# A recurrent layer and an attention layer on one core: the order in the last pass of a group of heads, and the place of the weight loads, changed

## The chip, the cores and the metric

The kernel runs on one core of a Trainium2 chip. The core has a matrix engine (PE, TensorE) that loads a 128x128 block of weights and streams up to 512 columns past it, a vector engine (DVE), a scalar engine for functions and casts (ACT), a general engine (POOL) and a sync engine (SP), which here issues all the transfers (DMAs). Each engine works through its own list of instructions in a fixed order, and an instruction that waits for a semaphore holds everything behind it on its engine. The metric is the device time of one execution in microseconds; less is better.

## The reference

One sequence of 1024 tokens with 1024 features goes through two layers with residuals: an RG-LRU layer and a layer of forgetting attention with 16 heads of 64 features, then a final norm. The change lies in the attention layer:

```python
def fox_mixer(h, w_in, b_f, w_out):
    u = h @ w_in
    q, k, v = (u[..., i * 1024:(i + 1) * 1024] for i in range(3))   # 16 heads x 64
    gate = u[..., 3 * 1024:4 * 1024]
    f_logit = u[..., 4 * 1024:] + b_f
    cum = cumsum(log_sigmoid(f_logit), axis=1)
    logits = q @ k.T / 8 + (cum_q - cum_k)       # for each head, causal mask
    p = softmax(logits)
    y = (p @ v) * silu(gate)
    return y @ w_out
```

All numbers are float32. The kernel gets that accuracy from three products of a reduced format: each operand is split into a high part (a cast) and a low part (what the cast left over), and high*high, low*high and high*low are added up in PSUM.

## The kernel before, in words

**Names.** A weight block is loaded from memory into a buffer `wf` (three such buffers exist), cast by ACT into its high part `wh`, and DVE subtracts to get the low part `wl`; after that the `wf` buffer is free again. `gps` are the products of the projections to queries, keys and gates (128 weights by 512 tokens), `vps` those of the values (128 tokens by 256 value columns, that is four heads), `S` the logits, `pt` transposed probabilities, and `O` the probabilities times the values. `ph` and `pl` are the high and low part of probabilities, `p` and `pp` rows of probabilities. Some of the probabilities are transposed on PE (`pt`); the others go out to memory and come back turned (`turnd<-turn`, then `pp<-turnd`), and their `ph` and `pl` are read from `pp`.

**Heads, passes and groups.** The attention runs head by head. Each head has two passes, for the two halves of the queries: `weigh(hd, 0)` runs beside `maxima(hd, 1)`, and `weigh(hd, 1)` beside `maxima(hd + 1, 0)`. `maxima` makes logits, masks them on DVE (line 775), and takes the exponential on ACT (line 780). `weigh` turns the probabilities, splits them and multiplies them with the values. Two heads are a pair, and share blocks of queries, keys and gates; four heads are a group, and share a block of values. While one pair is worked on, the projections of the next pair are made as a filling: `kq_units` for queries and keys and `g_units` for gates, through `project`, which makes four steps of six products for each half of the tokens. In the last head of a group (heads 3, 7 and 11) the values of the next group are prepared: `value_weights` loads and splits their weights, and `values` makes 192 products.

**The order.** Strings of digits and dots set it: a digit takes a step of one of the two passes, a dot takes a step of the filling (`fill`) and one of the small side work (`side`). The first pass of a head has five dots and the second six; heads 12 to 15 use longer strings (`LAST`). What is left of the filling is taken when the pass is over. The strings give each instruction its place in the program, and some instructions get an explicit "issue after". A scheduler with a model of the times then sets the real order on each engine: it moves what has no such tie, such as loads, weight splits and products of the values, to where its model finds the engine idle.

```python
ORDER = "1.0..1.10.1.0", "10..1.0.10.10.0"
LAST = "1..0.1..10..1..0", "10..1.0..10..1.0..0"
...
            run(second, weigh(hd, 1), maxima(hd + 1, 0), fill=fill, side=side)
            drain(side)
...
            if hd < 12:
                drain(fill)
            if hd % 4 == 3 and hd < 12:
                drain(values(hd // 4 + 1, parts))
```

Of the kernel before, what the change touches and what calls it, by code (L numbers as in the profile page):

```python
# [17 lines left out]
P = 128  # L18
# [20 lines left out]
def trunk(ctx: ExitStack, tc: tile.TileContext, xt, w0, wg, wo0, pc, gn, gf, w1, wv, wf, bf, wo1, out):  # L39
# [73 lines left out]
    def weights(src, parts=wpool, lo_eng=nc.gpsimd):  # L113

        for k in range(0, src.shape[1], 4):
            n = min(4, src.shape[1] - k)
            yield from split_weights([(src[:, k : k + n], slice(0, P))], (n, P), nc.scalar, lo_eng, parts)

    def gemm_steps(ps, pairs, chunks=(slice(0, HALF),)):

        pairs = list(pairs)
        for cs in chunks:
            o = ps[:, cs]
            for i, ((wh, wl), (xh, xl)) in enumerate(pairs):
                matmul(o, wh, xh[:, cs], start=i == 0, stop=False)
                matmul(o, wl, xh[:, cs], start=False, stop=False)
                matmul(o, wh, xl[:, cs], start=False, stop=i == len(pairs) - 1)
                if i % 2:
                    yield

    def drain(gen):
        for _ in gen:
            pass
# [368 lines left out]
    with ExitStack() as l1:  # L502
# [14 lines left out]
                    nc.vector.memset(f32(u[64:, 1]), 0.0)  # L517
                    nc.vector.memset(f32(u[64:68, 1]), -1.0)

        def project(w, use, hs=(0, 1)):  # L520

            for h in hs:
                pt = ps.tile([P, HALF], F32, tag="g", name="gps1")
                yield from gemm_steps(pt, zip(w, hT[h]))
                use(h, pt)

        def value_weights(g, parts):
# [20 lines left out]
        def values(g, parts):  # L548

            ex = 0 if g else HEADS  # L550
            for k in range(0, 0 if g else KT, 2):
                src = [(wv[g, :, k : k + 2], slice(0, 256)), (wf[:, k : k + 2], slice(256, 256 + ex))]
                parts += split_weights(src, (2, 256 + ex), nc.scalar, nc.gpsimd)
                if k == 2:
                    yield
            Vs[2 * g], Vs[2 * g + 1] = [], []
            for st in range(8):
                if ex and st % 2:
                    pt = ps.tile([P, SEQ], F32, tag="S", name="vps")[:, : 256 + ex]
                else:  # L560
                    pt = ps.tile([P, 256 + ex], F32, tag="g", name="vps")
                c = (st % 4) * P
                for k in range(KT):
                    xh, xl = hT[st // 4][k]
                    wh, wl = parts[k]
                    xh, xl = xh[:, c : c + P], xl[:, c : c + P]
                    matmul(pt, xh, wh, start=k == 0, stop=False)
                    matmul(pt, xl, wh, start=False, stop=False)
                    matmul(pt, xh, wl, start=False, stop=k == KT - 1)
                    if k % 4 == 1:  # L570
                        yield
                r_ = rms1[st // 4][:, st % 4 : st % 4 + 1]
                for a in range(2):
                    v = vpool.tile([P, 4, HD], F32R, tag=f"v{st}", name=f"v{st}", bufs=2)
                    src = pt[:, a * P : (a + 1) * P].rearrange("p (b d) -> p b d", b=2)
                    to_hi(v[:, 0::3], src, nc.scalar, scale=r_)
                    nc.vector.scalar_tensor_tensor(v[:, 1:3], src, r_, f32(v[:, 0::3]), ALU.mult, ALU.subtract)
                    Vs[2 * g + a].append(v)
                if ex:
                    nc.vector.tensor_scalar(fz[:, st], pt[:, 256:], r_, None, ALU.mult)  # L580
# [7 lines left out]

        kqw = {}

        def low(pair):
            return nc.vector if pair else nc.gpsimd

        def kq_units(pair, parts=((1, (0, 1)), (0, (0, 1)))):

            for is_k, hs in parts:
                if hs[0] == 0:
                    kq[pair, is_k] = tuple(
                        kqpool.tile([P, SEQ], F32R, tag=f"qk{p}{is_k}", name=f"qk{p}") for p in "hl"
                    )  # L600
                if hs[0] == 0 or pair == 0:
                    kqw[is_k] = list(weights(w1[is_k * 8 + pair], lo_eng=low(pair)))
                hi, lo = kq[pair, is_k]
                eng = nc.vector if pair == 0 else nc.scalar

                def use(h, pt):
                    cs = halves[h]
                    nc.vector.tensor_tensor(pt, pt, rs1[h], ALU.mult)
                    if is_k:
                        to_hi(hi[:, cs], pt, eng)  # L610
                        to_lo(lo[:, cs], pt, hi[:, cs], nc.vector)
                    else:
                        to_hi(hi[:, cs], pt, eng, scale=0.125)
                        nc.vector.scalar_tensor_tensor(lo[:, cs], pt, 0.125, f32(hi[:, cs]), ALU.mult, ALU.subtract)

                yield from project(kqw[is_k], use, hs)

        def load(hd, cs=slice(0, SEQ), us=(0, 1)):

# [72 lines left out]
        def g_units(pair, hs=(0, 1)):  # L692

            if hs[0] == 0:
                sgs[pair] = at.tile([P, SEQ], F32, tag="sg", name="sg1")
                gw[0] = list(weights(w1[16 + pair], lo_eng=low(pair)))
            sg = sgs[pair]

            def use(h, pt):
                g_ = sg[:, h * HALF : (h + 1) * HALF]  # L700
                nc.vector.tensor_tensor(g_, pt, rs1[h], ALU.mult)
                t = at.tile([P, HALF], F32, tag="xp", name="t1", bufs=2)
                nc.scalar.activation(t, g_, AF.Tanh, scale=0.5)
                nc.vector.scalar_tensor_tensor(g_, t, 1.0, g_, ALU.add, ALU.mult)

            yield from project(gw[0], use, hs)

        stats, ps_ = {}, {}

# [244 lines left out]
        def beside(*gens):  # L954
            for _ in itertools.zip_longest(*gens):
                yield
# [5 lines left out]
        def chain(*gens):  # L962
            for g in gens:
                yield from g
# [11 lines left out]
        def run(order, *gens, **kw):  # L976

            ordered(order, *gens, **kw)
            for g in gens:
                drain(g)  # L980
# [146 lines left out]
        for hd in range(HEADS):  # L1127
            pair = hd // 2
            if hd % 2 == 0:
                if hd < 12:  # L1130
                    fill = kq_units(pair + 1, ((1, (0, 1)), (0, (0,))))
                elif hd == 12:
                    pairs = ((0, 1), (2, 3), (4, 5), (6, 7))
                    todo = [(db, c) for two in pairs for c in range(2) for db in two]
                    fill = chain(
                        kq_units(7),
                        g_units(7, (0,)),
                        load_y(0),
                        first_out(),
                        g_units(7, (1,)),  # L1140
                        load_y(1),
                        partial(todo),
                        turned(0, 0),
                        turned(0, 1),
                    )
            elif pair < 6:
                fill = chain(kq_units(pair + 1, ((0, (1,)),)), late_q(hd + 1), g_units(pair + 1))
            first, second = LAST if hd > 11 else ORDER
            side = put_away(hd - 1) if 0 < hd < 13 else iter(())
            if hd % 4 == 3 and hd < 12:  # L1150
                parts = []
                coming = value_weights(hd // 4 + 1, parts)
                side = beside(side, itertools.islice(coming, 5))
            run(first, weigh(hd, 0), maxima(hd, 1), fill=fill, side=side)
            drain(side)
            if hd == HEADS - 1:
                break
            if hd == 14:
                with tc.issue_after(seen[0].ins):
                    split_y(1, 6, yos[6, 1])  # L1160
                scale(hd)
            side = late() if hd == 14 else settle(hd)
            if hd % 4 == 3 and hd < 12:
                side = beside(side, coming)
            run(second, weigh(hd, 1), maxima(hd + 1, 0), fill=fill, side=side)
            drain(side)
            if hd > 11:
                gated(hd, 1)
            if hd == 13:
                with tc.issue_after(seen[0].ins):  # L1170
                    split_y(0, 6, yos[6, 0])
            if hd < 12:
                drain(fill)
            if hd % 4 == 3 and hd < 12:
                drain(values(hd // 4 + 1, parts))
            if hd + 2 < HEADS:
                load(hd + 2, us=(0,) if hd % 2 == 0 and hd < 12 else (0, 1))
        quarters = [slice(0, 256), slice(256, HALF)]
# [83 lines left out]
```

## Time and profile before

| what | us |
|---|---|
| median of 3 runs (lowest, highest) | 1113.85 (1109.61, 1116.99) |
| the profiled execution, its own time | 1113.33 |
| its span, from the first instruction to the last | 1111.6 |
| PE busy with products | 1088.2 |
| PE busy with loading weights, beside the products | 921.9 |
| DVE busy | 785.4 |
| ACT busy | 581.3 |
| POOL busy | 175.2 |

The attention's heads begin at about 520 us of the span and end near 1050; the last passes of the three groups lie at about 604 to 647, 747 to 790 and 889 to 931 us. The 1.7 us between the profiled execution's own time and its span lie before the first and after the last instruction.

A row of the timeline gives the start in us from the span's beginning, the duration, the engine, the source line, the operation, what is written and read, the shape, how many such instructions were merged, and in brackets the idle time of the engine before it with what ended it. Most products show line 57, most casts line 87, most subtractions line 98, because helpers record them. PE overlaps its products, so that the duration of one (0.39 us for 512 columns) is longer than the distance to the next (0.23 us): the distance between two starts is what a product costs. A row of the windows gives the stretch in us, then its length, the busy time of PE, weight loading, DVE, ACT and POOL with the number of their instructions, the granted clock of PE as a share of the full one, the busy share of the DMA engines, and GB/s.

### The profile page before, as it was taken

The page shows a single profiled execution, that of the slowest core. Times are in us where ns is not written, and L with a number is a line of the kernel's source. Part 1 is how long each engine was busy: PE and PEld are TensorE (multiplying, and loading weights), DVE is VectorE, ACT ScalarE, POOL GpSimd, SP SyncE. Part 2 cuts the span into 40 slices and gives each one's busy share as a digit, 9 for nine tenths or more (in the row PEclk, how much of TensorE's full clock was granted, in tenths as well). Part 3 has the DMA queues.
Part 4 walks back from the last instruction along what each step waited for, and adds up shares of the span by engine and source line. Part 5 has one row for each costly group of instructions (what it writes and reads, how often), then busy time and mean ns, then how long its engine had stood idle before and what let it go on. Part 6 is the DMA issues. An engine that isn't in the chain of part 4 may idle for free.

```text
span 1111.6 us, 15903 instructions
## 1 busy us (share of the span) xinstructions
PE 1088.2 (98%) x5645; PEld 921.9 (83%) x5645; DVE 785.4 (71%) x1280; ACT 581.3 (52%) x1037; POOL 175.2 (16%) x120
## 2 busy tenths in 40 slices
PE   9999999999999999999999999999999999999997
PEld 7787888888888888988888888888888889888876
DVE  7888755876568687757788477875678765666645
ACT  8487345355453665545555355553555544444435
POOL 2322212111212201420010200202002020110110
PEclk9999999999999999999999999999999999999999
DMA  6111111111112113446767347675376763885445
GB/s 220 62 52 43 51 54 48 43 54 45 49 45 75 48 55 127 130 113 165 199 204 195 116 139 195 198 198 146 107 204 195 202 170 100 251 294 182 138 148 189
DMA packets 100919, 145.81 MB, mean 131 GB/s; under 512 B 25348, under 2 KB 53636, under 8 KB 100840
## 3 DMA queue, kind: packets, MB, share of 16 engines
q1 hardware_dynamic: 100840, 144.80, 44.2%
q8 instruction: 44, 0.72, 0.3%
q14 instruction: 35, 0.29, 0.1%
HBM read 83.48 MB, written 36.11 MB: 108 GB/s over the span
## 4 chain that ended last, share of the span: by engine, by line
PE 75%; DMA 8%; DVE 7%; issue 5%; ACT 3%; SPq 1%; POOL 1%; ACTq 0%; DVEq 0%; POOLq 0%
PE gps L57 24%; PE ops L57 16%; PE ups L57 10%; PE vps L57 8%; PE O L57 5%; PE S L57 4%; PE gate L57 3%; PE turn L57 2%; DMA pp<-turnd 2%; PE pt L61 2%; DMA wf<-in_w 2%; DVE pl L98 2%; DMA turnd<-turn 1%; DVE turn L735 1%; DVE S L775 1%
## 5 line engine op out<-in xcount | busy, mean ns | idle before, releaser
L57 PE MATMUL gps<-hh,wh 128*128 128x512 f32 x576 | 229.8, 399 | 0.3 <-ACT wh L87 0.3
L57 PE MATMUL gps<-hh,wl 128*128 128x512 f32 x576 | 226.2, 393 | 0.0
L57 PE MATMUL gps<-hl,wh 128*128 128x512 f32 x576 | 225.3, 391 | 0.0
L87 ACT CAST wh<-wf 128x512 fp32r<-128x512 f32 (+2 forms) x156 | 94.5, 610 | 152.6 <-PE gps L57 47.8
L98 POOL TENSOR_TENSOR wl<-wf,wh 128x512 fp32r<-128x512 f32 (+1 forms) x60 | 101.9, 1705 | 376.0 <-ACT wh L87 261.4
L57 PEld LDWEIGHTS gps<-hl,wh 128*128 128x128 f32 x576 | 108.5, 188 | 23.5
L57 PEld LDWEIGHTS gps<-hh,wl 128*128 128x128 f32 x576 | 108.8, 189 | 19.6 <-POOL wl L98 0.2
L57 PEld LDWEIGHTS gps<-hh,wh 128*128 128x128 f32 x576 | 108.7, 189 | 19.4 <-ACT wh L87 0.6
L815 POOL TENSOR_TENSOR sg<-sg,recb 64x512 f32<-64x512 f32 x32 | 44.1, 1397 | 494.9 <-DMA recb<-recd 494.9
L775 DVE CUSTOM_DVE_ANT_0 S<-S,mask 128x512 f32<-128x512 f32 (+7 forms) x128 | 97.1, 758 | 25.4 <-PE S L57 24.9
L780 ACT ACTIVATE pp<-S,m 128x512 f32<-128x512 f32 (+1 forms) x64 | 54.4, 850 | 76.8 <-DVE m L775 76.3
L57 PE MATMUL S<-T,U 128*128 128x512 f32 (+7 forms) x384 | 91.4, 346 | 0.0
L57 PE MATMUL O<-pl,v 128*128 128x256 f32 (+3 forms) x302 | 80.3, 301 | 10.8 <-DVE pl L98 10.5
L98 DVE TENSOR_TENSOR wl<-wf,wh 128x512 fp32r<-128x512 f32 x96 | 64.9, 677 | 30.7 <-ACT wh L87 30.5
L375 DVE TENSOR_TENSOR x<-x,ops 128x512 f32<-128x512 f32 x80 | 54.1, 680 | 40.7 <-PE ops L57 40.7
L57 PE MATMUL O<-ph,v 128*128 128x256 f32 (+3 forms) x302 | 80.1, 289 | 1.3 <-ACT ph L87 1.3
L57 PEld LDWEIGHTS S<-T,U 128*128 128x128 f32 (+1 forms) x384 | 68.2, 189 | 12.6 <-ACT pp L780 0.6
L57 PE MATMUL ups<-hh,wl 128*128 128x512 f32 x192 | 75.3, 392 | 0.8 <-POOL wl L98 0.8
L57 PE MATMUL ups<-hh,wh 128*128 128x512 f32 x192 | 75.5, 394 | 0.4 <-ACT hh L89 0.4
L57 PE MATMUL ops<-yh,wh 128*128 128x512 f32 x192 | 75.2, 392 | 0.0
L57 PE MATMUL ups<-hl,wh 128*128 128x512 f32 x192 | 75.1, 391 | 0.1
L57 PE MATMUL ops<-yh,wl 128*128 128x512 f32 x192 | 74.7, 389 | 0.0
(170 smaller groups left out, 2361.8 us busy)
## 6 DMA issues: line engine op xcount, KB each, us to landing
wf<-in_w SPq DMA_DIRECT2D x100, 256.0 KB
turnd<-turn SPq DMA_DIRECT2D x26, 448.0 KB
pp<-turnd SPq DMA_DIRECT2D x52, 224.0 KB
wf<-in_wo SPq DMA_DIRECT2D x64, 128.0 KB
U<-qkh SPq DMA_DIRECT2D x64, 128.0 KB
T<-qkh SPq DMA_DIRECT2D x28, 256.0 KB
turnd<-turn SPq DMA_DIRECT2D x13, 384.0 KB
pp<-turnd SPq DMA_DIRECT2D x52, 96.0 KB
```

The costliest lines, as they stand in the source:

```text
L57: pe[0] = nc.tensor.matmul(*args, **kw)
L61: pe[0] = nc.tensor.transpose(*args)
L87: nc.scalar.copy(hi, src)
L98: return eng.tensor_tensor(lo, src, f32(hi), ALU.subtract)
L375: nc.vector.tensor_tensor(x, x, pt, ALU.add)
L735: nc.vector.transpose(t[:, 0 if c else r].rearrange("p (m k q) -> p k m q", m=4, q=32), p[:, :n].rearrange("p (k m q) -> p k m q", m=4, q=32),
L775: masked[0] = nc.vector.tensor_tensor_reduce(S[:, :n], S[:, :n], mask[:, SEQ - n :], -1.0, -NEG, ALU.add, ALU.min, accum_out=m)
L780: seen[0] = nc.scalar.activation(p, S[:, :n], AF.Exp, bias=m, scale=-1.0, accum_out=sums[:, i : i + 1])
L815: nc.gpsimd.tensor_tensor(sg, sg, recs[hd // 2][rows, part], ALU.mult)
```

## The change

It has two parts. In heads 3, 7 and 11, the products of the values of the next group are no longer taken after the second pass, but chained behind the filling, and that pass uses the string with ten dots in the place of the one with six. And the weights of the projections, which were loaded and split in the step that uses them, are now loaded by `fetch_w`, which `project` calls on its last half behind the six products of the first of its four steps; the split follows three steps later, in `split_w`. Pair 0 keeps its old way (`i % 8 == 0`). `fetch_w` takes two of the three `wf` buffers at once. What is computed is unchanged.

```diff
+        loaded = {}
+        def fetch_w(i):
+            if i in loaded or i % 8 == 0:
+                return
+            loaded[i] = [wpool.tile([P, HALF], F32, tag="wf", name="wf", bufs=3) for _ in range(2)]
+            for k, a in enumerate(loaded[i]):
+                nc.sync.dma_start(a.rearrange("p (k j) -> p k j", k=4), w1[i, :, 4 * k : 4 * k + 4])
+        def split_w(i):
+            if i % 8 == 0:
+                return list(weights(w1[i], lo_eng=nc.gpsimd))
+            fetch_w(i)
+            w = []
+            for a in loaded.pop(i):
+                b, c = (wpool.tile([P, HALF], F32R, tag=t, name=t) for t in ("wh", "wl"))
+                to_hi(b, a, nc.scalar)
+                to_lo(c, a, b, nc.vector)
+                w += [(b[:, j : j + P], c[:, j : j + P]) for j in range(0, HALF, P)]
+            return w
-        def project(w, use, hs=(0, 1)):
+        def project(w, use, hs=(0, 1), following=0):
             for h in hs:
                 pt = ps.tile([P, HALF], F32, tag="g", name="gps1")
-                yield from gemm_steps(pt, zip(w, hT[h]))
+                for i, _ in enumerate(gemm_steps(pt, zip(w, hT[h]))):
+                    if i == 0 and h == hs[-1]:
+                        fetch_w(following)
+                    yield
                 use(h, pt)
...
-                    kqw[is_k] = list(weights(w1[is_k * 8 + pair], lo_eng=low(pair)))
+                    kqw[is_k] = split_w(is_k * 8 + pair)
...
-                yield from project(kqw[is_k], use, hs)
+                yield from project(kqw[is_k], use, hs, pair and (0 if hs == (0,) else pair if is_k else 16 + pair))
...
-                gw[0] = list(weights(w1[16 + pair], lo_eng=low(pair)))
+                gw[0] = split_w(16 + pair)
...
-            yield from project(gw[0], use, hs)
+            yield from project(gw[0], use, hs, 9 + pair if 0 < pair < 7 else 0)
...
             if hd % 4 == 3 and hd < 12:
                 side = beside(side, coming)
+                fill, second = chain(fill, values(hd // 4 + 1, parts)), LAST[1]
             run(second, weigh(hd, 1), maxima(hd + 1, 0), fill=fill, side=side)
...
-            if hd % 4 == 3 and hd < 12:
-                drain(values(hd // 4 + 1, parts))
```

In the built program every instruction of before is there after too, POOL's order is the same, and the other orders differ in three places only, once for each group, from head 2 (6, 10) to the end of head 3 (7, 11).

The first place is SP in the last pass of the first group. `pp_5197<-turnd1` are the four loads of the turned rows that this pass needs; `wf_5787` and `wf_5793` before, `wf_5421` and `wf_5422` after, are the two halves of the next key weights, called K0 and K1 below, and `wf_5985` (`wf_5890`) is the first half of the query weights behind them. Before:

```order
L747 DMA pp_5197<-turnd1_4012 32x8x224 x4
L625 DMA T1_3593<-qkl_4872 64x1024
L626 DMA T1_3593<-cumd_3584 2x1024
L634 DMA U1_3596<-qkh_5069 64x512
L635 DMA U1_3596<-qkh_5069 64x512
L636 DMA U1_3596<-qkl_5070 64x512
L796 DMA recd_3585<-rc_5345 8x128
L637 DMA U1_3596<-cumd_3584 2x512
L108 DMA wf_5787<-in_w1 128x512
L108 DMA wf_5793<-in_w1 128x512
L108 DMA wf_5985<-in_w1 128x512
L742 DMA turnd0_4011<-turn_5356 128x768
```

After, the same stretch of SP reads so (source lines are those of the changed file):

```order
L770 DMA pp_5197<-turnd1_4012 32x8x224 x4
L528 DMA wf_5421<-in_w1 128x512
L648 DMA T1_3593<-qkl_4876 64x1024
L649 DMA T1_3593<-cumd_3584 2x1024
L657 DMA U1_3596<-qkh_5073 64x512
L658 DMA U1_3596<-qkh_5073 64x512
L528 DMA wf_5422<-in_w1 128x512
L819 DMA recd_3585<-rc_5345 8x128
L659 DMA U1_3596<-qkl_5074 64x512
L660 DMA U1_3596<-cumd_3584 2x512
L528 DMA wf_5890<-in_w1 128x512
L765 DMA turnd0_4011<-turn_5356 128x768
```

K0 moved up past seven transfers, K1 past three.

The second place is ACT in the same pass, from the last rows of `maxima` on. `wh_5788` (after: `wh_5791`) is the cast of K0, `wh_5794` (`wh_5795`) that of K1; the four `ph<-pp` casts feed the last `O` products of the pass, `t1` belongs to the gates, and `v0` is the first block of the next values. Before:

```order
L780 ACTIVATE pp_5354,sums_5348<-S_5398,m_5401 128x384
L87 CAST wh_5788<-wf_5787 128x512
L780 ACTIVATE p_5450,sums_5348<-S_5445,m_5448 128x256
L87 CAST ph_5452<-pp_5197 128x8x2x32
L87 CAST ph_5454<-pp_5197 128x8x2x32
L780 ACTIVATE p_5475,sums_5348<-S_5470,m_5473 128x128
L89 ACTIVATE v0_5538<-vps_5513,rms10_3281 128x2x64
L87 CAST ph_5477<-pp_5197 128x8x2x32
L87 CAST ph_5479<-pp_5197 128x256
L89 ACTIVATE v0_5541<-vps_5513,rms10_3281 128x2x64
L87 CAST wh_5794<-wf_5793 128x512
```

After:

```order
L803 ACTIVATE pp_5354,sums_5348<-S_5398,m_5401 128x384
L87 CAST wh_5791<-wf_5421 128x512
L803 ACTIVATE p_5460,sums_5348<-S_5455,m_5458 128x256
L87 CAST ph_5462<-pp_5197 128x8x2x32
L87 CAST ph_5464<-pp_5197 128x8x2x32
L87 CAST wh_5795<-wf_5422 128x512
L726 ACTIVATE t1_5481<-sg1_5294 128x512
L803 ACTIVATE p_5496,sums_5348<-S_5491,m_5494 128x128
L87 CAST ph_5510<-pp_5197 128x8x2x32
L87 CAST ph_5512<-pp_5197 128x256
L89 ACTIVATE v0_5534<-vps_5484,rms10_3281 128x2x64
L89 ACTIVATE v0_5537<-vps_5484,rms10_3281 128x2x64
```

K0's cast keeps its place; K1's cast and the gates' `t1` now stand ahead of the last two `ph` casts, and the values' `v0` behind them. DVE's order follows: after the second `pl` come the last mask, K1's `wl`, the gates' `sg`, the last two `pl`, and then `v0`.

PE's products in this pass, from the end of its first eight `O` products on, stood so before: 6 gps, 16 vps, 2 S, 4 O, 6 gps, 2 S, 8 vps, 8 O, 6 gps, 6 O, and the rest of the vps. After: 12 gps, 2 S, 4 O, 6 gps, 6 vps, 2 S, 12 vps, 8 O, 24 vps, 6 O with one or two vps among them, and the rest of the vps.

The third place is ACT in the second pass of head 2 (6, 10), which makes the split of the second half of the gate weights: `wh_5298<-wf_5297` before, `wh_5299<-wf_5210` after. Before:

```order
L780 ACTIVATE pp_5019,sums_5013<-S_5014,m_5017 128x512
L87 CAST qkh_4871<-gps1_4969 128x512
L87 CAST wh_5298<-wf_5297 128x512
L780 ACTIVATE pp_5019,sums_5013<-S_5054,m_5057 128x384
L87 CAST ph_5092<-pt_5094 128x512
```

After:

```order
L803 ACTIVATE pp_5023,sums_5017<-S_5018,m_5021 128x512
L87 CAST wh_5299<-wf_5210 128x512
L87 CAST qkh_4875<-gps1_4969 128x512
L803 ACTIVATE pp_5023,sums_5017<-S_5058,m_5061 128x384
L87 CAST ph_5092<-pt_5094 128x512
```

The cast moved ahead of `qkh`. On SP the two loads of the gate weights have taken the places of the first two loads of the value weights, and these the places of the gates': the load that this cast needs stood behind the `y1d` writes of head 2's first pass, and stands now ahead of that pass's first turned row.

More of the change, by code (lines that the diff above doesn't have):

```diff
@@ L589, in trunk @@
         kqw = {}
-        def low(pair):
-            return nc.vector if pair else nc.gpsimd
         def kq_units(pair, parts=((1, (0, 1)), (0, (0, 1)))):
```

## The prediction

> **What bounds the kernel now.** I read the chain of waits first:
>
> ```profile
> span 1111.6 us, 15903 instructions
> PE 75%; DMA 8%; DVE 7%; issue 5%; ACT 3%; SPq 1%; POOL 1%; ACTq 0%; DVEq 0%; POOLq 0%
> ```
>
> PE sets the end. The change neither adds nor removes a product, so it can only win the time in which PE stands still at the places where the orders differ. Next the timeline of PE, from the first gps product behind the eight O products of a group's last pass to the first product of the unbroken run of vps: two rows for each of the three groups, and between those of the first the rows that price a product and show stops.
>
> ```profile
> 611.31 0.40 PE L57 MATMUL gps<-hh,wh 128*128 128x512 f32 x1
> 611.54 0.40 PE L57 MATMUL gps<-hh,wl 128*128 128x512 f32 x1
> ...
> 612.70 0.28 PE L57 MATMUL vps<-wh,hh 128*128 128x256 f32 x1
> 612.81 0.28 PE L57 MATMUL vps<-wh,hl 128*128 128x256 f32 x1
> ...
> 618.87 0.39 PE L57 MATMUL O<-ph,v 128*128 128x256 f32 x1 [0.81 <-ACT ph L87]
> 619.59 0.38 PE L57 MATMUL O<-pl,v 128*128 128x256 f32 x1 [0.34 <-DVE pl L98]
> ...
> 625.16 0.28 PE L57 MATMUL vps<-wh,hh 128*128 128x256 f32 x1
> ...
> 753.99 0.40 PE L57 MATMUL gps<-hh,wh 128*128 128x512 f32 x1
> ...
> 766.99 0.36 PE L57 MATMUL vps<-wh,hh 128*128 128x256 f32 x1
> ...
> 895.89 0.40 PE L57 MATMUL gps<-hh,wh 128*128 128x512 f32 x1
> ...
> 907.25 0.35 PE L57 MATMUL vps<-wh,hh 128*128 128x256 f32 x1
> ```
>
> By the distance of their starts a product of 512 columns costs 0.23 us and one of 256 about 0.12. Each stretch holds 18 gps, and 24 vps, 4 S and 18 O (all counted at 0.12): 18 x 0.23 + 46 x 0.12 = 9.66 us. The stretches took 13.85, 13.00 and 11.36 us. PE lost 4.19, 3.34 and 1.70 us, together 9.2.
>
> Part of the first loss is a slow clock, as the windows show (busy times of PE, weight loading, DVE, ACT, POOL, then the granted clock):
>
> ```profile
> 618.00:622.00 4.00, 2.12 (x11) 1.66 (x11) 3.15 (x6) 3.23 (x10) 3.05 (x2) 0.85 0.56 163
> 622.00:624.30 2.30, 2.30 (x8) 1.83 (x7) 2.30 (x3) 0.00 (x0) 1.97 (x2) 0.53 0.71 179
> 761.00:767.00 6.00, 4.40 (x23) 3.29 (x23) 5.35 (x9) 3.17 (x9) 3.60 (x3) 1.00 0.65 178
> ```
>
> PE was busy for 2.12 of 4.00 us, and ran at 0.53 of its clock in the 2.30 us behind it, a loss of 2.30 x 0.47 = 1.1 us; with 4.40 of 6.00 us the clock stayed at 1.00. It goes with the stop that called it.
>
> What PE waits for there is followed back in the timelines of ACT, DVE, POOL and SP:
>
> ```profile
> 615.96 0.62 ACT L87 CAST wh<-wf 128x512 fp32r<-128x512 f32 x1 [4.20 <-DMA wf<-in_w]
> 617.74 0.48 ACT L780 ACTIVATE p<-S,m 128x256 f32<-128x256 f32 x1 [1.16 <-DVE m L775]
> ...
> 618.21 1.13 ACT L87 CAST ph<-pp 128x512 fp32r<-128x512 f32 x2
> ```
>
> ```profile
> 616.61 0.69 DVE L98 TENSOR_TENSOR wl<-wf,wh 128x512 fp32r<-128x512 f32 x1 [3.93 <-ACT wh L87]
> 617.22 0.42 DVE L775 CUSTOM_DVE_ANT_0 S<-S,mask 128x256 f32<-128x256 f32 x1
> ...
> 618.85 0.69 DVE L98 TENSOR_TENSOR pl<-pp,ph 128x512 fp32r<-128x512 f32 x1 [1.14 <-ACT ph L87]
> ...
> 619.66 1.57 DVE L98 TENSOR_TENSOR pl<-pp,ph 128x512 fp32r<-128x512 f32 x1
> 621.15 0.34 DVE L577 SCALAR_TENSOR_TENSOR v<-vps,rms,v 128x128 fp32r<-128x128 f32 x1
> 621.41 2.92 DVE L98 TENSOR_TENSOR pl<-pp,ph 128x512 fp32r<-128x512 f32 x2
> ```
>
> ```profile
> 618.95 3.42 POOL L815 TENSOR_TENSOR sg<-sg,recb 64x512 f32<-64x512 f32 x2 [26.89 <-DMA recb<-recd]
> ```
>
> ```profile
> 577.72 0.47 SPq L108 DMA_DIRECT2D wf<-in_w  x1
> ...
> 603.88 3.13 SPq L747 DMA_DIRECT2D pp<-turnd  x4
> 607.06 0.61 SPq L625 DMA_DIRECT2D T<-qkl  x1
> ...
> 611.53 1.89 SPq L108 DMA_DIRECT2D wf<-in_w  x3
> ```
>
> SP issues K0, the next key weights, at 611.53; ACT, idle since 611.76, can cast it at 615.96; DVE's wl of it stands ahead of the next mask, which so starts at 617.22, the exponential behind it at 617.74, the ph casts at 618.21, and PE's O at 618.87. A load for work that is not due stands at the head of ACT's and DVE's lists. The waits in the other two groups' stretches are the same:
>
> ```profile
> ACT wh L87 <- DMA wf<-in_w: 3.9, 1, 3.9
> ...
> ACT wh L87 <- DMA wf<-in_w: 3.2, 1, 3.2
> ```
>
> **The change part by part.** *K0's load moves up.* It now stands right behind the four loads of pp, where T<-qkl stood at 607.06; its buffer has been free since the split of the second value weights. From issue to ACT's start it took 611.53 to 615.96, 4.43 us. From 607.06 that gives 611.49, before the 611.76 at which ACT asks. So the 4.20 us of waiting go; 615.96 is reached again only with a load of 8.9 us.
>
> *What is late next.* The mask then waits for PE's S, which stands behind 12 gps and no vps: 611.31 + 12 x 0.23 + 2 x 0.12 = 614.31. Mask 0.42, its read-out (some 0.14), exponential 0.48, two ph in 1.13: 616.5. Behind S, PE has 4 O, 6 gps, 6 vps, 2 S and 12 vps, 24 x 0.12 + 6 x 0.23 = 4.26 us, and asks for the first far O at 618.57. DVE's two pl and the gates' sg between them are ready at about 616.5 + 2 x 0.69 = 617.9. That is 0.7 us to spare, where PE now waits 0.81.
>
> *The second half of the pass.* DVE still has a mask (0.42 at most), K1's wl, sg and two pl, 0.42 + 4 x 0.69 = 3.18 us, to 621.1. PE beside it has 8 O and 24 vps, 32 x 0.12 = 3.84 us, to 622.4: 1.3 to spare, if DVE is undisturbed. It is not: while POOL ran, from 618.95 on, a pl took 1.57 and two took 2.92. With all four subtractions and sums at 1.5 DVE would end at 617.9 + 0.42 + 6.0 = 624.3, 1.9 late; with half of them, 622.7, 0.3 late. The Trainium skill's page "SBUF — State Buffer" (section "Who interferes with whom") says that DVE, with two operands in SBUF, and POOL, reading SBUF, lock each other out for whole instructions. The rows agree: the v at 621.15, with one operand in PSUM, kept its 0.34. By that rule all four would be held where POOL runs without a pause, and the sum is the second rival's.
>
> I take 0.4 for this and 0.4 for restarts like the 0.34 in the row at 619.59: 0.8 a group. The last passes give 9.2 - 3 x 0.8 = 6.8 us, between 9.2 and 9.2 - 3 x 1.9 = 3.5.
>
> *K1's cast now stands ahead of two ph casts,* a new place to wait. Its load is behind two of U, so issued near 609.9 (607.06 plus K0's share of the 1.89 for three, 0.63, plus some 2.2 for the transfers between), and there at 614.3 by the same 4.43; ACT comes to it at 616.5. No cost up to 2.2 us of delay, and 1.3 more on PE. Queued on SP behind K0 are T, U, recd, the turned row and recb; each moves by 0.63 us at most and is read in a later pass, or, as recb, only by POOL.
>
> *Heads 2, 6 and 10.* The second half of the gate weights kept ACT waiting there too:
>
> ```profile
> 582.22 0.62 ACT L87 CAST wh<-wf 128x512 fp32r<-128x512 f32 x1 [1.60 <-DMA wf<-in_w]
> ```
>
> Its load, at 577.72, took 4.50 us; it now goes out a pass earlier. From the first 256-wide S of a second pass to its last six O products took, in head 0, where no load is late, and in heads 2 and 6:
>
> ```profile
> 554.65 0.40 PE L57 MATMUL S<-T,U 128*128 128x256 f32 x2
> ...
> 560.14 0.28 PE L57 MATMUL O<-ph,v 128*128 128x256 f32 x1
> ...
> 583.65 0.39 PE L57 MATMUL S<-T,U 128*128 128x256 f32 x2
> ...
> 589.74 0.28 PE L57 MATMUL O<-ph,v 128*128 128x256 f32 x1
> ...
> 726.16 0.50 PE L57 MATMUL S<-T,U 128*128 128x256 f32 x2
> ...
> 732.43 0.28 PE L57 MATMUL O<-ph,v 128*128 128x256 f32 x1
> ```
>
> That is 5.49, 6.09 and 6.27 us. 0.60 and 0.78 go, and head 10 I take like head 6: 2.2 us, bounds 0 and 2.2; I take 2.0. The value weights that changed places with these loads have at least a pass until their split, so they cost nothing.
>
> *All else* keeps its order: the weight loads of the other heads were issued as early before, as far as three buffers let them. 0 us.
>
> The sum: 6.8 + 2.0 = 8.8 us off the profiled execution's 1113.33 (1.7 of which lie outside its span, unchanged): 1104.5. That execution lies 0.5 below the median, so 1104.5 counts as it stands.
>
> **The rivals.** *First, the loads are late in their new place too.* K0 follows four transfers of 224 KB that went out from 603.88 on. For it: the DMA engines are at 0.56 to 0.71 of their time even behind this stretch. Against: the load at 577.72 also followed four loads of pp, and took 4.50. It decides at K0's landing: up to some 7 us nothing changes, at 8.9 the last passes gain nothing and only heads 2, 6 and 10 do, 1111.3; beyond, each microsecond is lost three times, since ACT, DVE and then PE stand behind it, and a stop like the one before 622 brings the slow clock, 1.1 us, in all groups and not in one. With 12 us: 1111.3 + 3 x 3.1 + 2 x 1.1 = 1122.8, slower than before. The skill's page "DMA: Bandwidth & Descriptors" (section "Queues, rings and completion order") says that one engine's descriptors are consumed in ring order. By that rule K0 waits for all of pp, and a landing at 8.9 is possible if pp is slow; the rows so far show 4.43 and 4.50. Chance 0.11, of which 0.04 for slower than before.
>
> *Second, POOL holds DVE in all three groups:* 1.9 us a group instead of 0.4. For it: the 1.57 and 2.92. Against: POOL's start hangs on recb, which does not come earlier than its turned row lets it, and the first of the four then runs ahead of it. 9.2 - 3 x 2.3 + 2.0 = 4.3 us: 1109.0. Chance 0.14.
>
> *Third, the change does not do what it says:* the loads move, but PE meets other waits of the same size. Only a small part is gained, 1112. The wait of 3.2 us in the third group, which cost PE 1.70, speaks for this. Against it are the covers worked out above. Chance 0.06.
>
> *Fourth, no restarts and no POOL:* 11.4 us, 1101.9, chance 0.07.
>
> **How the numbers follow.** The forecast, 1104.5, has 0.62, with its own range of 1102 to 1107.5. A measurement can tell about 1% from no change, 11.1 us: below 1102.7 is faster, above 1125.0 slower. Of the forecast 0.17 lie below 1102.7, and the fourth rival's 0.07: faster 0.24. Slower is the first rival with the longest loads: 0.03. The same: 0.73. For the range, the fourth rival's 1101.9 less 2 for runs below the median (they went down to 1109.61 against 1113.85), and up over the second rival and the first's 1111.3 to the third's 1112: 1100 to 1112.
>
> **What would show it.** In the profile after, ACT's wh of K0 should have no wait for wf<-in_w in the last passes, and the six waits (three of 1.6 to 1.8, three of 3.2 to 4.2) be gone from the list; the stretch of PE should take about 10.5 us in each group; the clock be 1.00 throughout the heads; and from S to O 5.5 us in heads 2, 6 and 10. Wrong would be a wait of ACT at K1, PE waiting for pl with POOL running beside it (second rival), or K0 landing later than 614.

## The result, and the profile after

The changed kernel takes 1101.0 us in the median of 4 runs (1100.03 to 1101.87), against 1113.63 for the kernel before beside it; the ratio is 0.9895, with a 95% interval of 0.9875 to 0.9914. The forecast was 1104.5 with a range of 1100 to 1112. The result lies inside that range, but below the 1102 to 1107.5 that the prediction gave to the forecast itself, and below its mark of 1102.7 for "faster": it had given 0.24 to that side and 0.73 to "the same". The profiled execution took 1101.87, its span 1100.1, 11.5 less than before. One run of an experiment below took 1337.97 us at a granted clock of 0.752, and the ratios leave it out.

The head of the page, and the chain of waits:

```profile
span 1100.1 us, 15900 instructions
...
PE 80%; DVE 6%; DMA 5%; issue 5%; ACT 2%; SPq 1%; POOL 1%; ACTq 0%; DVEq 0%; POOLq 0%
```

DMA's share of the chain fell from 8 to 5%, and PE's rose from 75 to 80%. These points say where the chain runs and not what was won: three of them would be 33 us, and the span is 11.5 us shorter. Next PE's timeline at the place that the prediction read: the first gps product behind eight O, and the first vps product behind the last O, for each of the three groups, and in the first group the far O products between.

```profile
611.37 0.40 PE L57 MATMUL gps<-hh,wh 128*128 128x512 f32 x1
...
618.60 0.28 PE L57 MATMUL O<-ph,v 128*128 128x256 f32 x1
618.72 0.28 PE L57 MATMUL O<-pl,v 128*128 128x256 f32 x1
...
622.66 0.28 PE L57 MATMUL O<-ph,v 128*128 128x256 f32 x1
622.78 0.28 PE L57 MATMUL vps<-wh,hh 128*128 128x256 f32 x1
622.90 0.28 PE L57 MATMUL O<-pl,v 128*128 128x256 f32 x1
...
623.50 0.28 PE L57 MATMUL vps<-wh,hl 128*128 128x256 f32 x1
...
749.32 0.40 PE L57 MATMUL gps<-hh,wh 128*128 128x512 f32 x1
...
761.45 0.28 PE L57 MATMUL vps<-wh,hl 128*128 128x256 f32 x1
...
887.21 0.40 PE L57 MATMUL gps<-hh,wh 128*128 128x512 f32 x1
...
899.34 0.28 PE L57 MATMUL vps<-wh,hl 128*128 128x256 f32 x1
```

Each stretch takes 12.13 us. It holds 43 vps now, 19 more than before, so that it should take 9.66 + 19 x 0.12 = 11.94. PE loses 0.19 us in each group, where it lost 4.19, 3.34 and 1.70. (The prediction's 10.5 us for the stretch was meant for 24 vps; without the 19 more, 12.13 - 2.28 = 9.85 are left.) No row between has a wait in brackets: the far O at 618.60 follows its neighbour 0.12 us behind, and so does the O with pl. The prediction had worked out 618.57 for this O.

In the other engines' timelines at the same place, first ACT in all three groups (the casts of K0, the next key weights, and the exponential behind the first), then DVE, POOL and SP:

```profile
612.96 0.62 ACT L87 CAST wh<-wf 128x512 fp32r<-128x512 f32 x1 [1.12 <-PE gps L57]
615.08 0.48 ACT L803 ACTIVATE p<-S,m 128x256 f32<-128x256 f32 x1 [1.50 <-DVE m L798]
...
751.84 0.62 ACT L87 CAST wh<-wf 128x512 fp32r<-128x512 f32 x1 [2.05 <-DMA wf<-in_w]
...
889.14 0.62 ACT L87 CAST wh<-wf 128x512 fp32r<-128x512 f32 x1 [1.47 <-DMA wf<-in_w]
```

```profile
614.56 0.43 DVE L798 CUSTOM_DVE_ANT_0 S<-S,mask 128x256 f32<-128x256 f32 x1 [0.25 <-PE S L57]
...
619.81 3.09 DVE L98 TENSOR_TENSOR pl<-pp,ph 128x512 fp32r<-128x512 f32 x2 [0.31 <-ACT ph L87]
```

```profile
619.62 3.00 POOL L838 TENSOR_TENSOR sg<-sg,recb 64x512 f32<-64x512 f32 x2 [27.09 <-DMA recb<-recd]
```

```profile
607.08 0.61 SPq L528 DMA_DIRECT2D wf<-in_w  x1
...
745.68 0.60 SPq L528 DMA_DIRECT2D wf<-in_w  x1
...
883.02 0.60 SPq L528 DMA_DIRECT2D wf<-in_w  x1
```

In the first group the mask starts at 614.56, not at 617.22, and waits for PE's S, no longer for ACT's cast. ACT waits 1.12 us there for something else, the products that still read the old wh. In the second and third group ACT still waits for the load, which takes 751.84 - 745.68 = 6.16 and 889.14 - 883.02 = 6.12 us from issue to use. In the second group, DVE and PE go on behind that cast like this:

```profile
752.49 0.69 DVE L98 TENSOR_TENSOR wl<-wf,wh 128x512 fp32r<-128x512 f32 x1 [1.78 <-ACT wh L87]
753.10 0.43 DVE L798 CUSTOM_DVE_ANT_0 S<-S,mask 128x256 f32<-128x256 f32 x1
```

```profile
752.07 0.40 PE L57 MATMUL S<-T,U 128*128 128x256 f32 x2
...
756.55 0.28 PE L57 MATMUL O<-ph,v 128*128 128x256 f32 x1
756.67 0.28 PE L57 MATMUL O<-pl,v 128*128 128x256 f32 x1
```

S is there at 752.47, but the mask has to wait for wl and starts at 753.10, some 0.6 us later than behind S in the first group. This delay reaches pl, which ends at 755.42, and not PE, which asks for it only at 756.67. In the third group the mask starts 0.04 us behind the end of S, as in the first. So the load is still late in two groups, and PE loses nothing by it.

The clock and the passes of heads 2 and 6 (from the first 256-wide S to the last six O, as in the prediction):

```profile
618.00:622.00 4.00, 4.00 (x36) 4.00 (x35) 3.69 (x7) 1.92 (x6) 2.38 (x2) 1.00 0.48 143
622.00:624.30 2.30, 2.30 (x21) 2.28 (x21) 1.51 (x3) 0.95 (x2) 1.98 (x2) 1.00 0.84 211
```

```profile
584.35 0.40 PE L57 MATMUL S<-T,U 128*128 128x256 f32 x2
...
589.81 0.28 PE L57 MATMUL O<-ph,v 128*128 128x256 f32 x1
...
722.29 0.40 PE L57 MATMUL S<-T,U 128*128 128x256 f32 x2
...
727.77 0.28 PE L57 MATMUL O<-ph,v 128*128 128x256 f32 x1
```

PE is busy throughout and its clock is full. The passes take 5.46 and 5.48 us, where they took 6.09 and 6.27; that of head 10 also went from 6.27 to 5.48.

Both traces hold 5645 products, so the time of the k-th one can be set against the k-th of before. That divides the whole difference:

| from | change, us |
|---|---|
| the start to the last pass of head 3 (start of the program +0.39, heads 1 and 2 -0.33) | +0.06 |
| last pass of head 3 | -4.0 |
| from there to the last pass of head 7 (head 6 in it) | -0.7 |
| last pass of head 7 | -3.2 |
| from there to the last pass of head 11 (head 10 in it) | -0.8 |
| last pass of head 11 | -1.6 |
| one wait near the end of the program | -1.2 |
| sum, before rounding | -11.5 |

The wait near the end is that of a product for DVE's `xp`, behind the attention, before and after:

```profile
1074.46 0.66 PE L57 MATMUL turn<-ident,x 128*128 128x128 f32 x4 [1.71 <-DVE xp L1016]
```

```profile
1063.01 0.66 PE L57 MATMUL turn<-ident,x 128*128 128x128 f32 x4 [0.48 <-DVE xp L1039]
```

In the profiles of the experiments below PE's order there is the same and it stops there for 0.5 to 1.4 us (1.87 by the distance of the starts in the kernel before, 0.65 in the changed one), without any connection with the edits. So the 1.2 us there, and the +0.39 at the start, are counted as differences between executions. The 10.7 us that are left belong to the stretch from head 1 to the last pass of head 11.

### The profile page after: what moved, and what is told of

It reads as the page before. It is cut to its first block, busy times and chain, and to the rows that moved or that the text cites. A ratio compares the mean times of both kernels' runs of the same rounds, so it can differ in the third digit from the quotient of the medians.

```text
span 1100.1 us, 15900 instructions
## 1 busy us (share of the span) xinstructions
PE 1082.6 (98%) x5645; PEld 919.9 (84%) x5645; DVE 782.1 (71%) x1280; ACT 583.1 (53%) x1037; POOL 172.9 (16%) x120
## 4 chain that ended last, share of the span: by engine, by line
PE 80%; DVE 6%; DMA 5%; issue 5%; ACT 2%; SPq 1%; POOL 1%; ACTq 0%; DVEq 0%; POOLq 0%
PE gps L57 27%; PE ops L57 17%; PE ups L57 10%; PE vps L57 9%; PE O L57 5%; PE S L57 4%; PE pt L61 3%; PE gate L57 3%; PE turn L57 3%; DMA pp<-turnd 1%; DVE pl L98 1%; DVE turn L758 1%; DMA turnd<-turn 1%; DVE gps L631 1%; DMA T<-qkh 1%
```

## The experiments

Two theories stood against each other. **Theory A:** the late load of K0 was the first cause, as the prediction says. **Theory B:** the string of ten steps does the work, and the load's wait only hid another. A second question was what POOL does to DVE.

**Only the weight loads moved.** The changed kernel, but the last pass of a group keeps the string with six dots, and the values' products come behind it. PE, ACT and DVE have the order of before in the last passes; SP has the order of after.

```diff
-                fill, second = chain(fill, values(hd // 4 + 1, parts)), LAST[1]
...
+            if hd % 4 == 3 and hd < 12:
+                drain(values(hd // 4 + 1, parts))
```

> Only the weight loads move ahead, as in the changed kernel; the last pass of a group keeps the string with six dots and the values' products come after it, so that PE, ACT and DVE keep the order of before there. Theory A (the key weights' late load was the first stop, and what POOL does to DVE the second): ACT's waits for wf<-in_w go in the last passes and in heads 2, 6 and 10. The stretch from S to O in heads 2, 6, 10 takes 5.5 us, 2.2 us won. In a last pass the first stop (0.97 and 0.61 us in the first group) goes; the second part still has the values' v ahead of ph, and pl at 1.5 us beside POOL: about 1.3 us stay in each group, 9.2 - 3.9 = 5.3 won. Together 7.5: about 1106. Theory B (the string of ten steps does the work, and the load's wait only hid another one): only the 2.2 us of heads 2, 6 and 10, about 1111.4.

Measured: 1101.75 us (1100.9 to 1102.23), ratio 0.9903 (0.9881 to 0.9924). The loads alone give nearly all of the gain. Theory B falls. Theory A was right in kind and missed in size: it had forecast about 1106, and left 4 us of the gain to the string. In this trace PE stops twice for 0.23 us in the first group, at 620.36 and just behind, since POOL began at 618.49 and DVE's last two pl ran beside it:

```profile
618.18 2.12 DVE L98 TENSOR_TENSOR pl<-pp,ph 128x512 fp32r<-128x512 f32 x2 [0.26 <-ACT ph L87]
```

The kernel was run once more together with the changed one:

> Only the weight loads moved, once more: 1101.5 to 1101.8 if the 0.46 us of stops at 620 us of its first trace are there in each execution and cost what they show; 1101.0 if not.

> The changed kernel as it is, beside the one with only its loads moved, to tell the two apart: 1101.0. If the string of ten steps is worth what the traces show, which is 0.6 us of stops in the first group's last pass and nothing in the others, it is 0.5 to 0.7 us below the other; if it is worth nothing, within 0.3.

Measured: 1102.67 (1102.17 to 1103.0) with only the loads, 1101.6 (1101.33 to 1102.76) for the whole change. Product by product the two traces differ by 0.2 us in the three last passes together; another 0.44 is the wait near the end of the program, which is no part of the change. In this trace the two stops in the first group aren't there. With them, the first trace of this kernel is 0.7 us behind the first of the changed one in the same passes. So the string of ten steps is worth 0.2 to 0.7 us by the traces and about 1 by the medians of the two kernels run side by side, whose ranges overlap; its exact worth is left open.

Why the six-dot pass stops no more shows in the first group's last pass, in the rows of ACT, DVE and POOL of this second run:

```profile
612.75 0.62 ACT L87 CAST wh<-wf 128x512 fp32r<-128x512 f32 x1 [1.12 <-PE gps L57]
```

```profile
618.96 1.03 DVE L98 TENSOR_TENSOR pl<-pp,ph 128x512 fp32r<-128x512 f32 x2 [0.26 <-ACT ph L87]
```

```profile
619.64 2.77 POOL L838 TENSOR_TENSOR sg<-sg,recb 64x512 f32<-64x512 f32 x2 [27.06 <-DMA recb<-recd]
```

The last two pl start at 618.96, and take 1.03 us together: the first of them is just over when POOL begins, and neither is held. In the kernel before they started at 621.41 and took 2.92. The late load had pushed DVE's last work into the time in which POOL works. The expectation had left it there.

**Only the string of ten steps.** The loads stay where before has them.

```diff
+                fill, second = chain(fill, values(hd // 4 + 1, parts)), LAST[1]
...
-            if hd % 4 == 3 and hd < 12:
-                drain(values(hd // 4 + 1, parts))
```

> Only the string with ten dots and the chained products of the values; the weight loads stay where before has them. Theory A: ACT still waits about 4 us for the first key weights in each last pass and 1.6 to 1.8 in heads 2, 6, 10. The mask still starts 1.2 us behind ACT's cast, PE asks for the far O at about 618.6 and stops for 0.3 and 0.6; behind it DVE has mask, wl, two sg steps and two pl, most of them at 1.5 us beside POOL, and PE stops for about 2 more: some 2.9 us a group against 4.2, 3.3 and 1.7 before. 0 to 2 us won: 1112 to 1113.6. Theory B: most of the gain, below 1106.

Measured: 1113.59 us (1111.33 to 1114.4), against 1111.93 for the kernel before beside it; ratio 1.0003 (0.999 to 1.0015). ACT's and PE's rows in the first group's last pass:

```profile
615.68 0.62 ACT L87 CAST wh<-wf 128x512 fp32r<-128x512 f32 x1 [4.39 <-DMA wf<-in_w]
```

```profile
618.58 0.38 PE L57 MATMUL O<-ph,v 128*128 128x256 f32 x1 [0.36 <-ACT ph L87]
...
619.30 0.39 PE L57 MATMUL O<-pl,v 128*128 128x256 f32 x1 [0.34 <-DVE pl L98]
...
621.00 0.39 PE L57 MATMUL O<-pl,v 128*128 128x256 f32 x1 [0.74 <-DVE pl L98]
```

The wait of 4.39 us is there, and PE stops three times behind it, as theory A has it. In the second and third group the new order does make the stretches shorter, by 1.7 and 1.0 us by the products' times, and PE gives that and a little more back right behind, in the second group here:

```profile
769.60 0.39 PE L57 MATMUL O<-pl,v 128*128 128x256 f32 x1 [1.44 <-DVE pl L98]
```

DVE's last wl, sg and the first of the last two pl took 1.66, 1.77 and 1.75 us there, all beside POOL, which began at 764.33. This is what the prediction's second rival describes, and it comes about here, with the load late. With the load late, the new string brings nothing; with the load early, hardly anything.

**The loads one step later.** The only size in the change is the step behind which the next weights are loaded.

```diff
-                    if i == 0 and h == hs[-1]:
+                    if i == 3 and h == hs[-1]:
```

> The changed kernel with one size different: the next weights are loaded behind the last of the four steps, not the first. In the built order this takes back the place of the gate weights in heads 2, 6 and 10 (loads behind the y1d writes, cast behind qkh) and nothing else; PE, and the last passes on every engine, keep the changed order. If the terms of the prediction are right, ACT waits 1.6 to 1.8 us for gate weights again, the stretch from S to O is 6.1 to 6.3 instead of 5.5, and the time is 2.2 us above the changed kernel's 1101.0: 1103.2. If the gain there belonged to something else, the time stays at 1101.0.

Measured: 1104.0 us (1103.65 to 1104.43), ratio 0.9925 (0.9908 to 0.9943), 3.0 above the first and 2.4 above the second measurement of the changed kernel. ACT waits for gate weights again in head 2, and PE for pl behind it:

```profile
582.36 0.62 ACT L87 CAST wh<-wf 128x512 fp32r<-128x512 f32 x1 [1.67 <-DMA wf<-in_w]
```

```profile
584.82 0.39 PE L57 MATMUL O<-pl,v 128*128 128x256 f32 x1 [0.36 <-DVE pl L98]
```

Product by product it loses 0.67, 0.84 and 0.65 us around heads 2, 6 and 10, 2.16 together, nothing in the last passes, and 0.73 in the wait near the end. The term for these heads holds.

**POOL's multiplication left out.** POOL doesn't multiply the gates of heads 0 to 11 by the reciprocal sums; the same edit in the changed kernel and in the kernel before.

```diff
-                nc.gpsimd.tensor_tensor(sg, sg, recs[hd // 2][rows, part], ALU.mult)
+                if hd > 11:
+                    nc.gpsimd.tensor_tensor(sg, sg, recs[hd // 2][rows, part], ALU.mult)
```

> The changed kernel without POOL's multiplication of the gates by the reciprocal sums in heads 0 to 11 (left out, to free POOL; the result lacks this factor). If POOL slows DVE where both run, the last two pl of a last pass take 0.69 and about 0.4 us instead of 1.65 and 1.51. Theory A: PE had 0.24 us of stop at most there, since its own work covers 1.5-us pl, so the time stays within 1 us of the changed kernel's: 1100 to 1101. The second rival (POOL holds DVE on the path): 2 us or more below. If the slow pl comes from something else, such as the DMA traffic, pl stays at 1.5.

> The kernel before without POOL's multiplication of the gates by the reciprocal sums in heads 0 to 11 (left out, to free POOL; the result lacks this factor). Theory A (POOL's hold on DVE made the second stop of the last passes): pl at 0.69 us, the second stops go (0.89 + 0.26 in the first group, 0.46 + 0.84 + 0.23 in the second, 0.45 + 0.23 in the third, 3.4 us together), and with less idle time in the first group perhaps the slow clock's 1.1: 1109 to 1110.5. The first stops (0.97 + 0.61, 0.70 + 0.60, 0.61), which go back to the key weights' load, stay. If POOL's part is nothing, the time stays at 1113.6.

Measured: 1101.55 us (1101.04 to 1102.53) from the changed kernel, and 1107.94 from the kernel before, whose runs beside it have a median of 1111.92: ratio 0.9962 (0.9944 to 0.998). The last two pl of the first group, in the one and in the other:

```profile
619.14 1.03 DVE L98 TENSOR_TENSOR pl<-pp,ph 128x512 fp32r<-128x512 f32 x2 [0.31 <-ACT ph L87]
```

```profile
620.98 1.03 DVE L98 TENSOR_TENSOR pl<-pp,ph 128x512 fp32r<-128x512 f32 x2 [0.16 <-ACT ph L87]
```

They take 1.03 us where they took 3.09 and 2.92, so that the slow pl do come from POOL; the DMA traffic is still there. In the changed kernel this is worth nothing, since PE's own work covers even the slow ones. In the kernel before it is worth 4 us by the medians, and 4.2 in the three last passes product by product, the slow clock's part included. What is left there belongs to the load, as ACT's row and the window show (PE's busy time is the first number behind the length, the granted clock the third from the end):

```profile
615.84 0.62 ACT L87 CAST wh<-wf 128x512 fp32r<-128x512 f32 x1 [4.35 <-DMA wf<-in_w]
```

```profile
618.00:622.00 4.00, 2.91 (x16) 2.46 (x17) 2.88 (x8) 3.01 (x10) 0.00 (x0) 1.00 0.65 178
```

The first stops, 1.12 and 0.61 us by the distance of the starts, are still there, the second ones are gone, and the clock stays full with PE at 2.91 of 4.00 us.

**Another string for the first passes.** The changed kernel still stops for 0.80 us in eight first passes, where DVE has other subtractions ahead of pl. Here both steps of filling stand ahead of the last row of maxima.

```diff
-ORDER = "1.0..1.10.1.0", "10..1.0.10.10.0"
+ORDER = "1.0..1.10..10", "10..1.0.10.10.0"
```

> The changed kernel with another string for the first pass of heads 0 to 11, 1.0..1.10..10 in the place of 1.0..1.10.1.0: both steps of filling stand ahead of the last row of maxima. In the changed kernel's trace PE stops for 0.80 us in eight first passes, where DVE has a weight split's wl, qkl and the mask of that last row ahead of the pl that PE asks for; in the new order pl stands ahead of this mask. If that stop is of the same kind as the ones removed, most of 8 x 0.8 = 6.4 us goes: 1095 to 1098. If the last row's own mask and exponential then come too late for the next pass, the stop only moves there: 1100 to 1103 or more.

Measured: 1108.85 us (1107.55 to 1109.58), ratio 0.9962 (0.9949 to 0.9976), some 7 slower than the changed kernel. The stop at pl goes, and a longer one comes at the start of the next pass, here in head 3:

```profile
606.32 1.09 PE L61 MATMUL pt<-ident,p 128*128 128x128 f32 x8 [1.11 <-ACT p L803]
```

The last row's exponential is now what PE waits for.

**One subtraction moved to POOL.** The low half of the stored rows of y goes from DVE to POOL.

```diff
-                to_lo(yo.bitcast(F32R), yo, yh, nc.vector)
+                to_lo(yo.bitcast(F32R), yo, yh, nc.gpsimd)
```

> The changed kernel with the low half of the stored rows of y (yo less yh, two per pair) subtracted on POOL, not on DVE. In the first pass of heads 2, 4, 6, 8 and 10 one of these, 0.65 us, stands ahead of the mask and the pl behind it that PE asks for, and PE stops for 0.80 us there. If the order on DVE is what the stops are made of, they shrink to the 0.2 us of heads 3, 7 and 11, where DVE has one subtraction less ahead: 5 x 0.6 = 3.0 us won, 1098. If POOL, working on these numbers just then, holds DVE's pl, whose operands both lie in SBUF, at 1.5 us instead of 0.69, this gives 0.8 a head back and the time is 1101 to 1102.

Measured: 1099.38 us (1098.8 to 1101.19), 2.2 below the changed kernel in the same comparison; the ratio to the kernel before is 0.9874 (0.9859 to 0.9889). It is the fastest of all. The same product in the first pass of head 6, first in the changed kernel, then here, with POOL's row of that time:

```profile
712.65 0.39 PE L57 MATMUL O<-pl,v 128*128 128x256 f32 x1 [0.65 <-DVE pl L98]
```

```profile
709.75 0.39 PE L57 MATMUL O<-pl,v 128*128 128x256 f32 x1
```

```profile
706.58 1.29 POOL L98 TENSOR_TENSOR yo<-yo,yh 128x512 fp32r<-128x512 f32 x1 [4.06 <-ACT yh L87]
```

The wait of 0.65 is gone. POOL was done at 707.87, before the pl of this pass, and held up nothing that PE waits for. All five stops went from 0.80 to 0.21 us, 3.0 together as expected; the medians show 2.2 of it.

## Why the prediction was right, and where it was off

**K0's load.** The step "so the 4.20 us of waiting go" was right for what matters, PE's stops, and the run with the loads alone shows that this step carries the result. Its size of the landing was off. The prediction took 4.43 us from issue to use, from the old place in the first group; in the second and third group the load at that place had taken 758.37 - 755.56 = 2.81 and 899.57 - 896.41 = 3.16 us, and it took 6.16 and 6.12 in the new place (in the first group the wait for wh hides it). The wait of ACT did not go there, it fell from 3.9 and 3.2 to 2.05 and 1.47. So of the six waits that should have been gone from the list, four are gone. What saved the forecast was the bound in its first rival, "up to some 7 us nothing changes": the mask came 0.6 us late in the second group, and the time that PE had to spare covered it. It was not far from the sign of being wrong: counted from the stretch's start, the two landings lie at 613.9 and 613.3 of the first group's time, and the prediction had named 614.

**The last passes.** The mis-sized term is "0.8 a group", 0.4 for POOL and 0.4 for restarts. By the products' times the last passes gained 8.8 us in place of 6.8, so that 0.4 was left in the three groups (0.6 by the stretches) and not 2.4. Two things failed in it. The first is POOL. It held only the last two pl, and only in the first group, 3.09 us for both; in the other groups it began during the last pl, at 758.56 and 896.45, and the two took 1.02 and 1.03. The prediction had DVE end at 622.7 with half of the four operations held, 0.3 after PE asks for the last six O. DVE ended at 622.90, but PE comes for the last pl only with the last O, at 623.38, so that there was time to spare. The second is the restarts. The 0.34 at 619.59 was no restart: its row names DVE's pl, which ran from 618.85 to 619.54 behind the late ph. It was the first stop handed on, and by the run with the loads alone it went with it.

**Heads 2, 6 and 10.** 2.0 was taken, with 2.2 as the upper bound; the passes became 0.63, 0.79 and 0.79 us shorter in heads 2, 6 and 10, and the run with the later loads gives 2.16 back. Right.

**The slow clock.** It was counted to the stop that called it and it went with it: 1.00 in both windows.

**The rivals.** The first, loads late in their new place, describes what happened to the load, but its point of 8.9 us was not reached. A load still later was not tried. The second is right as a mechanism, and worth 4 us in the kernel before, where the late load had brought DVE's work into POOL's time; after the change they meet too little to matter. The third fell. The fourth, no restarts and no POOL, is close to what came about and had a chance of only 0.07: the waits were added up as if each group were the first. That its 1101.9 meets the profiled 1101.87 so well is in part luck, since 0.8 of the 11.5 us come from the start and from the wait near the end.

**The sum.** 6.8 + 2.0 = 8.8 were forecast. The last passes gave 8.8, heads 1, 2, 6 and 10 together 1.8, and the start and the wait near the end another 0.8 that no edit explains: 11.5 before rounding. What the prediction did not say is that one of the change's two parts would have done.

Two statements ahead of the result were wrong in their words and change no number: both strings of ORDER have six dots, and the undisturbed pass at 554.65 is head 1's, not head 0's.

## What to carry to other kernels

Where engines work through fixed lists, look for the load that stands at the head of one and isn't due: its lateness is handed on from ACT to DVE to PE, and moving one issue up by 4.5 to 5.2 us was worth more here than a new order of the products, which without it was worth nothing. Price a delay also by what it pushes the work into: some 4 us of the loss came from DVE's last steps sliding into POOL's time. When a load has moved, its own time may grow; the bound that matters is when its user is really needed, not when it asks.

## What the runs showed of the hardware

DVE's subtractions with both operands in SBUF took 1.03 us for two without POOL's multiplication, and 3.09 and 2.92 beside it, while the v operation with an operand in PSUM kept 0.34. This agrees with the rule that the prediction took from the Trainium skill's page "SBUF — State Buffer" (section "Who interferes with whom"), and two runs now have its price on the path: 4 us of 1111.92 in the kernel before, none in the changed one.

A load of 256 KB took 4.4 to 4.5 us from issue to use where the prediction read it, 2.8 and 3.2 at the same place in the second and third group, and 6.1 to 6.2 there in its new place, right behind four loads of the turned rows. That these four loads are the reason was not tested.

The clock fell to 0.53 in the kernel before after 4.00 us in which PE was busy for 2.12; with 2.91 of 4.00, without POOL's multiplication, it stayed at 1.00. With only the string of ten steps PE was busy for 2.56 us of the same stretch, and the clock fell too:

```profile
618.00:622.00 4.00, 2.56 (x16) 1.95 (x16) 3.44 (x6) 2.95 (x8) 3.25 (x2) 0.96 0.61 170
622.00:626.00 4.00, 4.00 (x24) 4.00 (x24) 3.56 (x6) 1.25 (x4) 1.70 (x2) 0.61 0.58 161
```

Where between 2.56 and 2.91 it decides, and whether the busy time of such a stretch alone decides it, isn't shown.
